# A float32 decoder trunk: all transfers other than weights, input and output issued from the POOL queue instead of SyncE's

## The chip, the cores and the metric

The kernel runs on one core of one Trainium2 chip. The metric is the device time in microseconds of one execution. Three runs of the kernel before the change are given; their median is 1368.77 us (1365.99 to 1369.58).

The core has five instruction queues that run beside each other and wait for one another by semaphores: TensorE (PE, with its weight loads shown as PEld), VectorE (DVE), ScalarE (ACT), GpSimd (POOL) and SyncE (SP), which does no arithmetic and only begins transfers. A transfer is begun by one of the queues and carried out by 16 DMA engines; a queue works in order, so an instruction that waits holds up what is behind it on the same queue.

## The reference

The kernel computes a decoder trunk of two layers over 512 tokens with 1024 features, all in float32. Cut to what matters:

```
def rms_norm(x, w, eps):  return x * rsqrt(mean(x*x, -1) + eps) * w

# layer 0: mixer
h = rms_norm(x, norm_mix[0])
u, q, k, v = split(h @ mix_w_in)                # 512 + 512 + 128 + 128 columns
pooled = [means over 2/4/8/16 trailing tokens of u, minus u] @ pool_w * pool_scale
attn = sliding_window_attention(rope(q), rope(k), v, sinks)     # window 128, 8 heads
x = x + concat(pooled, attn) @ mix_w_out
x = x + conv_ffn(rms_norm(x, norm_ffn[0]))      # (silu(conv(h@up_g)) * conv(h@up_u)) @ down

# layer 1: state space
h = rms_norm(x, norm_mix[1])
z, xbc, dt = split(h @ ssm_w_in)                # xbc: causal convolution of width 4, silu
y = ssd_scan(xs, softplus(dt + bias), -exp(A_log), B, C) + D * xs    # chunks of 128 tokens
x = x + rms_norm(y * silu(z), ssm_norm) @ ssm_w_out
x = x + conv_ffn(rms_norm(x, norm_ffn[1]))
out = rms_norm(x, norm_final)
```

## The kernel before, in words

Everything is kept with the features on the 128 partitions and the 512 tokens along the rows. The residual stream `x` stays in the core's memory as eight tiles of 128x512.

A float32 product is made from exact halves. `load_split` (L131 to L141) loads a weight tile `w` of 128x1024 (512 KB) from SyncE's queue, ScalarE rounds it to `wh` (L139) and VectorE takes the rest `wl` (L140); three buffers are kept of each. `gemm` then issues three matmuls for each of the eight slices (L147 to L149) into one of four PSUM banks with the tag `mm`: 24 matmuls for a tile of 128 features by 512 tokens.

The norm's scale for each token is not needed for a product's inputs. It is applied to the product's result, so the matmuls can run ahead of it. `Stat.add` has ScalarE square a tile and POOL add it up (L172, L173). `Stat.finish` makes the sums over the features by TensorE (L180) and the reciprocal root by a few short VectorE instructions (L184 to L190). The result `rt` holds the tokens along the partitions, 128x4. To get it along the rows on all partitions, `finish` writes it to device memory (`flat<-rt`, L193, 128x4 single elements) and reads it back to all 128 partitions (`rb<-flat`, L195). Six statistics take this way, in order of time: ahead of the mixer, ahead of the first MLP, ahead of the state-space layer, for the norm of y, ahead of the second MLP, and for the first half of the tokens in the final norm. The second half in the final norm takes another way, by TensorE (L199). VectorE multiplies the products by `rb` (L227, L233), which empties the `mm` banks.

The mixer's rotary tables (`rope_tables`) are computed from the positions `pos`, and four copies `L<-L` (L333) spread cosines and sines over the partitions of the two heads. `rope` exchanges halves of a head by four copies `sq<-p` (L356) for the keys and the first two query tiles, by a TensorE product for the others. POOL multiplies by the cosines (L360), VectorE by the sines (L361) and adds (L362). `poolw` (L340) holds the pooling group's weights.

The state-space layer first computes the step sizes (weights `wd`, L514) and the sums over a chunk, and writes these to device memory (`scr`, L564). Then it goes through eight groups; each has six projections of 24 matmuls and a scan over four chunks. Each chunk reads its rows of `scr` to all partitions into `R` (L631, 256 KB, three buffers; `poolw` and the keys use these buffers earlier). VectorE subtracts and clips (L634), ScalarE takes exponentials, POOL multiplies by C (L641) and TensorE sums (L645, L648).

The order of the instructions on each queue is not written by hand. The program is traced once and a planner orders it with a simulated timeline of all queues (`schedule_with_timeline_sim=True`), earlier instructions of the program first where several are ready.

Of the kernel before, what the change touches and what calls it, by code (L numbers as in the profile page):

```python
# [20 lines left out]
P = 128  # L21
# [10 lines left out]
EPS = 1e-6  # L32
SSM_EPS = 1e-5

# columns of the packed per-feature parameters
C_NMIX = 0
C_NFFN = 16
C_NFIN = 32
# [6 lines left out]
C_SD = C_SNW + 16  # L45
NPAR = C_SD + 16

# columns of the constants
K_ID = 0
K_TRI = 128  # L50
K_ONE = 256
# [18 lines left out]
def trunk_kernel(ctx: ExitStack, tc: tile.TileContext, io):  # L70
    nc = tc.nc
    V, A, G, PE = nc.vector, nc.scalar, nc.gpsimd, nc.tensor
# [32 lines left out]
    def yps():  # L105
        return pp.tile([P, T], F32, tag="yp", name=nm("yp"), bufs=2)

# [1 line left out]
    x = cp.tile([P, KD, T], F32, name="x")  # L109
    par = cp.tile([P, NPAR], F32, name="par")  # L110
    con = cp.tile([P, NCON], F32, name="con")
    row = cp.tile([P, 72], F32, name="row")
    nc.sync.dma_start(par[:, :C_NFFN], io["par"][:, :C_NFFN])
    nc.sync.dma_start(x[:, 0, :], io["xT"][:, 0, :])
    # the array's clock and the activation table are up by the time the data is there
    idle = t2("sq", 2)
    G.memset(idle[:], 1.0)
    A.activation(idle[:, 0:1], idle[:, 1:2], AF.Copy)
# [8 lines left out]
    def pc(c):  # L127
        return par[:, c : c + 1]

# [1 line left out]
    def load_split(src, kt=8, cols=P, eng=None):  # L131
        w = wp.tile([P, 8, P], F32, tag="w", name=nm("w"), bufs=3)
        h = wp.tile([P, 8, P], F32R, tag="wh", name=nm("wh"), bufs=3)
# [19 lines left out]
        V.scalar_tensor_tensor(out=l, in0=src, scalar=wcol, in1=h.bitcast(F32),  # L153
                               op0=ALU.mult, op1=ALU.subtract)

# [1 line left out]
    class Stat:  # L157
        def __init__(self, count, width=T, lanes=(G,), late=0):
            self.n, self.w, self.lanes, self.late = 0, width, lanes, count - late
# [15 lines left out]
        def finish(self, dim, eps, copy=True):  # L175
            w, nb = self.w, self.w // P
            ps = aux()
            for c in range(nb):
                for i, part in enumerate(self.parts):
                    PE.matmul(ps[:, c : c + 1], lhsT=part[:, c * P : (c + 1) * P], rhs=ones[:, 0:1],  # L180
                              start=i == 0, stop=i == len(self.parts) - 1)
            sm = tp.tile([P, 4, NB], F32, tag="rt", name=nm("rt"), bufs=2)
            v, s, r, q = (sm[:, i, :nb] for i in range(4))
            V.tensor_scalar(v, ps[:, 0:nb], 1.0 / dim, eps, op0=ALU.mult, op1=ALU.add)  # L184
            A.activation(s, v, AF.Sqrt)
            V.reciprocal(r, s)
            V.tensor_tensor(out=q, in0=r, in1=r, op=ALU.mult)
            V.tensor_tensor(out=q, in0=q, in1=v, op=ALU.mult)
            V.tensor_scalar(q, q, -0.5, 1.5, op0=ALU.mult, op1=ALU.add)
            V.tensor_tensor(out=r, in0=r, in1=q, op=ALU.mult)  # L190
            if copy:
                flat = dp.tile([NB, P], F32, tag="flat", name=nm("flat"), bufs=2)
                nc.sync.dma_start(flat[:nb, :].rearrange("c p -> p c"), r)  # L193
                rb = t2("rb", 1)
                nc.sync.dma_start(rb[:, :w], flat[:nb, :].rearrange("c p -> (c p)").partition_broadcast(P))  # L195
                return rb, r
            pb = aux()
            for c in range(nb):
                PE.matmul(pb[:, c * P : (c + 1) * P], lhsT=r[:, c : c + 1].to_broadcast([P, P]), rhs=ident,  # L199
                          start=True, stop=True)  # L200
            if not copy:
                return pb, r
            rb = t2("rb", 1)
            A.activation(rb[:, :w], pb[:, :w], AF.Copy)
            return rb, r
# [27 lines left out]
        V.tensor_tensor(out=out, in0=ps, in1=rb[:], op=ALU.mult)  # L233

    def conv(src, dst, taps, b):
        """dst = causal depthwise convolution of src; taps oldest first, as columns of par."""
        A.activation(dst, src, AF.Identity, scale=pc(taps[-1]), bias=pc(b))  # L237
        for s in range(1, len(taps)):
            V.scalar_tensor_tensor(out=dst[:, s:], in0=src[:, : T - s], scalar=pc(taps[-1 - s]),  # L239
                                   in1=dst[:, s:], op0=ALU.mult, op1=ALU.add)  # L240

# [1 line left out]
    def finish_out(down, nj, kh, kl):  # L243
        H = T // 2
        warm = tp.tile([P, 1], F32, tag="warm", name="warm", bufs=1)
# [16 lines left out]
                                       in1=scale[half][:, :H], op0=ALU.mult, op1=ALU.mult)  # L262
                nc.sync.dma_start(io["out"][k * P : (k + 1) * P, ts], x[:, k, ts])

# [1 line left out]
    def ffn(layer, cur, nxt):  # L266
        rb, _ = cur.stat.finish(D, EPS)
        up, down = io["wup"], io["wdn"]
# [39 lines left out]
                if part == len(FF_PARTS) - 1:  # L308
                    nxt.tile(n)

# [1 line left out]
    def rope_tables(rb):  # L312
        """The cosines (upper rows) and signed sines (lower rows) of a head, times the tokens' scale."""
        pos = t2("p", 3, I32)
        nc.sync.dma_start(pos[:], io["pos"].partition_broadcast(P))
        ang, n, r = t2("acc", 3), t2("p", 3), t2("L", 3)
        phase, shift, sign = (con[:, K_PH + i : K_PH + i + 1] for i in range(3))
        V.tensor_copy(ang[:], pos[:])
        V.tensor_scalar(ang[:], ang[:], con[:, K_INVF : K_INVF + 1], 0.0, op0=ALU.mult, op1=ALU.add)
        V.tensor_scalar(n[:], ang[:], INV2PI, phase, op0=ALU.mult, op1=ALU.add)  # L320
        V.tensor_scalar(n[:], n[:], MAGIC, MAGIC, op0=ALU.add, op1=ALU.subtract)
        V.scalar_tensor_tensor(out=r[:], in0=n[:], scalar=-PI_C1, in1=ang[:], op0=ALU.mult, op1=ALU.add)
        V.scalar_tensor_tensor(out=r[:], in0=n[:], scalar=-PI_C2, in1=r[:], op0=ALU.mult, op1=ALU.add)
        V.scalar_tensor_tensor(out=r[:], in0=n[:], scalar=-PI_C3, in1=r[:], op0=ALU.mult, op1=ALU.add)
        V.tensor_scalar(r[:], r[:], shift, PI_LIM, op0=ALU.add, op1=ALU.min)
        V.tensor_scalar(r[:], r[:], -PI_LIM, 0.0, op0=ALU.max, op1=ALU.add)
        A.activation(r[:], r[:], AF.Sin, scale=sign)
        V.tensor_tensor(out=r[:], in0=r[:], in1=rb[:], op=ALU.mult)
        res = []
        for half in range(2):  # L330
            t = t2("L", 3)
            for head in range(2):
                nc.sync.dma_start(t[64 * head : 64 * head + 64, :], r[64 * half : 64 * half + 64, :])  # L333
            res.append(t)
        return res

# [1 line left out]
    def mixer(cur, nxt, first_ws):  # L338
        poolw = tp.tile([P, 4, P], F32, tag="R", name="poolw", bufs=3)
        nc.sync.dma_start(poolw[:], io["poolw"])  # L340
        rb, rt = cur.stat.finish(D, EPS)
        hp, lp, ha, la = bt(), bt(), bt(), bt()

# [6 lines left out]
        def rope(ps, dst, by_dma):  # L350
            f = t2("p", 3)
            A.activation(f[:], ps[:], AF.Copy)
            if by_dma:
                src = t2("sq", 2)
                for b in range(4):
                    nc.sync.dma_start(src[32 * b : 32 * b + 32, :], f[32 * (b ^ 1) : 32 * (b ^ 1) + 32, :])  # L356
            else:
                src = yps()
                PE.matmul(src[:], lhsT=swap, rhs=f[:], start=True, stop=True)
            G.tensor_tensor(out=dst[:], in0=f[:], in1=cos[:], op=ALU.mult)  # L360
            V.tensor_tensor(out=f[:], in0=src[:], in1=sin[:], op=ALU.mult)  # L361
            V.tensor_tensor(out=dst[:], in0=dst[:], in1=f[:], op=ALU.add)  # L362

        # causal pooling
        def pool(g, w):
            ps = project(g)
            ub = ct()
# [18 lines left out]
        cos, sin = rope_tables(rb)  # L386
        k = ct()
        rope(project(8), k, True)
        # each key head alone, the other's rows zero, so that the products span all rows
        kz = [tp.tile([P, T], F32, tag="R", name=nm("kz"), bufs=3) for _ in range(2)]  # L390
        for p in range(2):
            rows, rest = slice(p * 64, (p + 1) * 64), slice((1 - p) * 64, (2 - p) * 64)
# [12 lines left out]
        for j in range(4):  # L405
            ps = project(4 + j)
            q.append(ct())
            rope(ps, q[j], j < ROPE_DMA)
        # banded attention, two heads groups of four; heads j and 4+j share tile j
        mask = con[:, K_MASK : K_MASK + 256]  # L410
        def scores(n):
            k0 = 0 if n else P
# [50 lines left out]
            A.activation(hh, o4, AF.Copy)  # L463
            V.tensor_tensor(out=ll, in0=o4, in1=hh.bitcast(F32), op=ALU.subtract)

        # the pooled half of the output product and the attention's first tokens run beside the attention
        def out_pooled(n2):
            ws = load_split(io["wmo"][0, n2])
            for i in range(2):
# [36 lines left out]
            out_attn(n, wa[n], slice(T // 2, T))  # L506
            nxt.tile(n)

# [1 line left out]
    def ssm(cur, nxt):  # L510
        rb, rt = cur.stat.finish(D, EPS)
        # step sizes, token-major [token, chunk, head]: four column groups, each over a quarter of the features
        wd = wp.tile([P, KD, NH], F32, tag="w", name="wd", bufs=3)
        nc.sync.dma_start(wd[:], io["wdt"])  # L514
        wn = par[:, C_NMIX + 8 : C_NMIX + 16].unsqueeze(2).to_broadcast([P, KD, NH])
        V.tensor_tensor(out=wd[:], in0=wd[:], in1=wn, op=ALU.mult)
        dfm = mm()
# [10 lines left out]
        dt, av, acs, dec, dbc, e1, e2 = (sd[:, i, :] for i in range(7))  # L528

        def v3(a):  # L530
# [3 lines left out]
        V.tensor_tensor(out=v3(dt), in0=v3(dt), in1=rt.unsqueeze(2).to_broadcast([P, NB, NH]), op=ALU.mult)  # L534
        V.tensor_tensor(out=v3(dt), in0=v3(dt), in1=row[:, 0:NH].unsqueeze(1).to_broadcast([P, NB, NH]),
                        op=ALU.add)
        # softplus(v) = max(v, 0) + 2 atanh(e / (2 + e)), e = exp(-|v|)
        A.activation(e1, dt, AF.Abs)
        A.activation(e1, e1, AF.Exp, scale=-1.0)
        V.tensor_scalar(e2, e1, 2.0, 0.0, op0=ALU.add, op1=ALU.add)  # L540
# [20 lines left out]
        A.activation(dbc, ps[:, P : 2 * P], AF.Exp)  # L561
        V.tensor_copy(e1, ps[:, 2 * P : 3 * P])
        scr = dp.tile([P, P], F32, name="scr")
        nc.sync.dma_start(scr[:], e1)  # L564

        stat = Stat(16)
        y4 = [bt(F32) for _ in range(4)]
# [16 lines left out]
        for g in range(GROUPS):  # L584
# [42 lines left out]
            for c in range(NB):  # L627
                cs = slice(c * P, (c + 1) * P)
                h0 = c * NH + 4 * g
                R = tp.tile([P, 4, P], F32, tag="R", name=nm("R"), bufs=3)  # L630
                nc.sync.dma_start(R[:], scr[h0 : h0 + 4, :].partition_broadcast(P))  # L631
                L = tp.tile([P, 4, P], F32, tag="L", name=nm("L"), bufs=3)
                for r in range(4):
                    V.tensor_scalar(L[:, r, :], R[:, r, :], acs[:, h0 + r : h0 + r + 1], 0.0,  # L634
# [26 lines left out]
            for t in range(2):  # L661
                f = 2 * g + t
# [107 lines left out]
```

## Time and profile before

| What | Value |
|---|---|
| Runs | 1365.99, 1368.77, 1369.58 us, median 1368.77 |
| Profiled execution | span 1366.1 us; its time outside the profile is not given apart from it |
| PE busy | 1311.2 us, 96% |
| DVE busy | 887.5 us, 65% |
| ACT busy | 597.5 us, 44% |
| POOL busy | 161.2 us, 12%, 117 instructions |
| Transfers | 134.30 MB, mean 98 GB/s, all from SyncE's queue |

The span is cut by a page into busy shares, a chain of work that ended last, groups of instructions by line, and transfers. In a group, `out<-in` are the program's names without buffer numbers. In a timeline, the columns are the start and the duration in us, the engine, the line and the operation; the bracket gives the idle time ahead of it and what ended that. "SPq" is SyncE's queue, whose rows are the issues of transfers; "issue" is time in which an engine waited for nothing that the profile shows. PEclk is the clock that was granted to TensorE, 1.00 being full speed.

### The profile page before, as it was taken

How to read it: one execution, taken by the hardware profiler on the slowest of the kernel's cores; microseconds unless marked ns; L12 is line 12 of the kernel's file. 1: busy time of each engine (PE TensorE's matmuls, PEld its weight loads, DVE VectorE, ACT ScalarE, POOL GpSimd, SP SyncE). 2: the span in 40 equal slices, each digit the busy share in tenths (PEclk: the TensorE clock that was granted, in tenths of full speed). 3: DMA queues.
4: the chain of work that ended last, by engine and by line, in shares of the span. 5: the costliest groups of instructions: out<-in, count | busy, mean ns of one | idle time of the engine just before them, and what ended most of it. 6: DMA issues, size and time to landing. Idle time of an engine off the chain costs nothing.

```text
span 1366.1 us, 16570 instructions
## 1 busy us (share of the span) xinstructions
PE 1311.2 (96%) x6398; PEld 1073.4 (79%) x6398; DVE 887.5 (65%) x1364; ACT 597.5 (44%) x826; POOL 161.2 (12%) x117
## 2 busy tenths in 40 slices
PE   8799999999999999899999999997999999999995
PEld 5576978888888887778888888676878888888895
DVE  5674548547646764678888878854567467557763
ACT  5364235324424443465666655632344234334451
POOL 3213020000000002012321313211100000000021
PEclk9899999999999999999999999999999999999998
DMA  6313113233233323253333333212333333233352
GB/s 223 103 37 93 63 39 119 93 103 102 81 105 104 95 88 102 70 132 109 100 109 103 98 120 97 91 64 85 93 87 97 102 99 96 92 101 103 96 155 81
DMA packets 46511, 134.30 MB, mean 98 GB/s; under 512 B 8160, under 2 KB 10592, under 8 KB 46432
## 3 DMA queue, kind: packets, MB, share of 16 engines
q1 hardware_dynamic: 46432, 133.25, 32.1%
q8 instruction: 50, 0.82, 0.2%
q14 instruction: 29, 0.24, 0.1%
HBM read 129.74 MB, written 2.17 MB: 97 GB/s over the span
## 4 chain that ended last, share of the span: by engine, by line
PE 85%; DMA 6%; DVE 4%; issue 2%; ACT 2%; POOL 0%; SPq 0%; DVEq 0%; ACTq 0%; POOLq 0%
PE mm L149 26%; PE mm L147 26%; PE mm L148 26%; DMA flat<-rt 3%; DMA rb<-flat 2%; DVE wl L140 1%; PE yp L645 1%; PE yp L453 1%; PE mm L420 1%; DMA R<-scr 1%; PE ax L459 1%; ACT wh L139 1%; PE yp L648 1%; PE ax L651 1%; DVE c L239 1%
## 5 line engine op out<-in xcount | busy, mean ns | idle before, releaser
L147 PE MATMUL mm<-a,wh 128*128 128x512 f32 x1232 | 486.4, 396 | 19.9 <-DVE p L227 7.8
L149 PE MATMUL mm<-a,wl 128*128 128x512 f32 x1232 | 486.6, 395 | 3.6 <-DVE wl L140 3.6
L148 PE MATMUL mm<-a,wh 128*128 128x512 f32 x1232 | 485.3, 394 | 3.4 <-DVE a L153 3.4
L139 ACT ACTIVATE wh<-w 128x1024 fp32r<-128x1024 f32 (+1 forms) x221 | 229.0, 1041 | 411.7 <-PE mm L148 366.4
L140 DVE TENSOR_TENSOR wl<-w,wh 128x1024 fp32r<-128x1024 f32 (+1 forms) x222 | 281.6, 1271 | 78.3 <-ACT wh L139 77.1
L147 PEld LDWEIGHTS mm<-a,wh 128*128 128x128 f32 x1232 | 233.3, 189 | 73.1 <-issue 21.8
L149 PEld LDWEIGHTS mm<-a,wl 128*128 128x128 f32 x1232 | 233.0, 189 | 56.8 <-DVE wl L140 6.7
L148 PEld LDWEIGHTS mm<-a,wh 128*128 128x128 f32 x1232 | 233.1, 189 | 56.3 <-DVE a L153 7.2
L173 POOL TENSOR_TENSOR sacc<-sacc,sq 128x512 f32<-128x512 f32 (+1 forms) x53 | 82.2, 1552 | 907.7 <-ACT sq L172 906.2
L233 DVE TENSOR_TENSOR p<-mm,rb 128x512 f32<-128x512 f32 x120 | 82.4, 689 | 100.2 <-PE mm L149 79.1
L239 DVE SCALAR_TENSOR_TENSOR acc<-p,par,acc 128x511 f32<-128x511 f32 (+1 forms) x176 | 131.1, 748 | 3.1 <-ACT acc L237 0.3
L149 PE MATMUL mm<-b,wl 128*128 128x512 f32 (+1 forms) x272 | 92.4, 344 | 6.1 <-DVE wl L140 6.1
L230 DVE TENSOR_TENSOR x<-mm,x 128x512 f32<-128x512 f32 x48 | 32.4, 689 | 98.0 <-PE mm L149 98.0
L148 PE MATMUL mm<-b,wh 128*128 128x512 f32 (+1 forms) x272 | 93.7, 346 | 0.0
L148 PE MATMUL mm<-c,wh 128*128 128x512 f32 x240 | 93.3, 390 | 0.0
L147 PE MATMUL mm<-b,wh 128*128 128x512 f32 (+1 forms) x272 | 92.0, 345 | 1.0 <-ACT wh L139 1.0
L147 PE MATMUL mm<-c,wh 128*128 128x512 f32 x240 | 92.3, 390 | 0.5 <-ACT c L152 0.5
L149 PE MATMUL mm<-c,wl 128*128 128x512 f32 x240 | 92.6, 389 | 0.0
L237 ACT ACTIVATE acc<-p,par 128x512 f32<-128x512 f32 x88 | 71.0, 809 | 31.1 <-DVE p L233 30.6
L239 DVE SCALAR_TENSOR_TENSOR c<-p,par,c 128x511 f32<-128x511 f32 (+2 forms) x96 | 75.3, 784 | 1.6 <-ACT c L237 0.4
L296 ACT ACTIVATE acc<-acc 128x512 f32<-128x512 f32 x44 | 27.8, 633 | 80.8 <-DVE acc L239 80.8
L149 PEld LDWEIGHTS mm<-b,wl 128*128 128x128 f32 x272 | 52.6, 194 | 12.1 <-DVE wl L140 6.3
(185 smaller groups left out, 1276.6 us busy)
## 6 DMA issues: line engine op xcount, KB each, us to landing
w<-wup SPq DMA_DIRECT2D x88, 512.0 KB, 3.5
w<-wsi SPq DMA_DIRECT2D x48, 512.0 KB, 3.5
w<-wdn SPq DMA_DIRECT2D x32, 448.0 KB, 3.2
w<-wdn SPq DMA_DIRECT2D x24, 512.0 KB, 3.5
R<-scr SPq DMA_DIRECT2D x32, 256.0 KB, 3.5
w<-wso SPq DMA_DIRECT2D x16, 512.0 KB, 3.6
w<-wmi SPq DMA_DIRECT2D x10, 512.0 KB, 4.0
w<-wmo SPq DMA_DIRECT2D x8, 512.0 KB, 3.5
```

Of the source, the lines that this page charges most:

```text
L139: A.activation(h[:, :kt, :cols], w[:, :kt, :cols], AF.Copy)
L140: V.tensor_tensor(out=l[:, :kt, :cols], in0=w[:, :kt, :cols], in1=h[:, :kt, :cols].bitcast(F32), op=ALU.subtract)
L147: PE.matmul(ps, lhsT=h[:, k, :], rhs=rh[k][:, ts], start=first and k == 0, stop=False)
L148: PE.matmul(ps, lhsT=h[:, k, :], rhs=rl[k][:, ts], start=False, stop=False)
L149: PE.matmul(ps, lhsT=l[:, k, :], rhs=rh[k][:, ts], start=False, stop=last and k == kt - 1)
L173: self.lanes[lane].tensor_tensor(out=acc[:, :w], in0=acc[:, :w], in1=sq[:, :w], op=ALU.add)
L230: V.tensor_tensor(out=x[:, n, :], in0=ps[:], in1=x[:, n, :], op=ALU.add)
L233: V.tensor_tensor(out=out, in0=ps, in1=rb[:], op=ALU.mult)
L237: A.activation(dst, src, AF.Identity, scale=pc(taps[-1]), bias=pc(b))
L239: V.scalar_tensor_tensor(out=dst[:, s:], in0=src[:, : T - s], scalar=pc(taps[-1 - s]), in1=dst[:, s:], op0=ALU.mult, op1=ALU.add)
L296: A.activation(g[:], g[:], AF.Silu)
L420: PE.matmul(s[:, j, k0:], lhsT=q[2 * jj + j][:, n * P : (n + 1) * P], rhs=kz[p][:, n * P + k0 - P : (n + 1) * P], start=True, stop=True)
```

## The change

Every transfer that isn't a weight tile of a large product, the input or the output is begun by POOL (`G.dma_start`) where it was begun by SyncE (`nc.sync.dma_start`). What stays on SyncE: all loads of `w`, the input `x`, the constants `con`, `par` and `row`, and the stores of `out`. The pieces below are the whole change; other differences are in comments only.

```diff
 # Stat.finish
-                nc.sync.dma_start(flat[:nb, :].rearrange("c p -> p c"), r)
+                G.dma_start(flat[:nb, :].rearrange("c p -> p c"), r)
                 rb = t2("rb", 1)
-                nc.sync.dma_start(rb[:, :w], flat[:nb, :].rearrange("c p -> (c p)").partition_broadcast(P))
+                G.dma_start(rb[:, :w], flat[:nb, :].rearrange("c p -> (c p)").partition_broadcast(P))
 # rope_tables
-        nc.sync.dma_start(pos[:], io["pos"].partition_broadcast(P))
+        G.dma_start(pos[:], io["pos"].partition_broadcast(P))
...
-                nc.sync.dma_start(t[64 * head : 64 * head + 64, :], r[64 * half : 64 * half + 64, :])
+                G.dma_start(t[64 * head : 64 * head + 64, :], r[64 * half : 64 * half + 64, :])
 # mixer, rope
-        nc.sync.dma_start(poolw[:], io["poolw"])
+        G.dma_start(poolw[:], io["poolw"])
...
-                    nc.sync.dma_start(src[32 * b : 32 * b + 32, :], f[32 * (b ^ 1) : 32 * (b ^ 1) + 32, :])
+                    G.dma_start(src[32 * b : 32 * b + 32, :], f[32 * (b ^ 1) : 32 * (b ^ 1) + 32, :])
 # ssm
-        nc.sync.dma_start(wd[:], io["wdt"])
+        G.dma_start(wd[:], io["wdt"])
...
-        nc.sync.dma_start(scr[:], e1)
+        G.dma_start(scr[:], e1)
...
-                nc.sync.dma_start(R[:], scr[h0 : h0 + 4, :].partition_broadcast(P))
+                G.dma_start(R[:], scr[h0 : h0 + 4, :].partition_broadcast(P))
```

## The prediction

> **What bounds the kernel now.** I read the page's busy shares first, then the chain that ended last, then TensorE's timeline for every idle stretch, the waits of the SyncE queue, and last the transfers.
>
> ```profile
> span 1366.1 us, 16570 instructions
> ...
> PE 1311.2 (96%) x6398; PEld 1073.4 (79%) x6398; DVE 887.5 (65%) x1364; ACT 597.5 (44%) x826; POOL 161.2 (12%) x117
> ```
>
> TensorE is busy 96% of the span: 1366.1 - 1311.2 = 54.9 us are idle. Nothing but that idle time, and TensorE's clock, can be won back; a delay elsewhere costs only where TensorE ends up waiting.
>
> ```profile
> 205.00:540.00 335.00, 335.00 (x1485) 276.07 (x1484) 214.09 (x267) 133.02 (x167) 10.98 (x7) 1.00 0.32 98
> ...
> 575.00:850.00 275.00, 271.95 (x1528) 223.22 (x1527) 227.58 (x413) 162.23 (x208) 64.19 (x38) 1.00 0.36 108
> ```
>
> The columns are the stretch, its length, and the busy time of PE, PEld, DVE, ACT and POOL. In the first stretch (all the gated MLP's inner part) PE is busy 335.00 of 335.00 us, in the second (most of the state-space scan) 271.95 of 275.00, at a granted clock of 1.00. Weights arrive in time there, so transfers taken off SyncE's queue free nothing.
>
> ```profile
> SPq L135 <- DVE wl L140: 915.3, 189, 21.3
> SPq L195 <- DMA flat<-rt: 49.1, 6, 9.3
> ```
>
> The queue of SyncE (SPq) spends 915.3 us waiting until a weight buffer is free, which no other queue changes. It stands 49.1 us, six times, behind `flat<-rt`: the same queue waits for that transfer before it may begin `rb<-flat`, and weight loads stand behind both.
>
> ```profile
> PE 85%; DMA 6%; DVE 4%; issue 2%; ACT 2%; POOL 0%; SPq 0%; DVEq 0%; ACTq 0%; POOLq 0%
> PE mm L149 26%; PE mm L147 26%; PE mm L148 26%; DMA flat<-rt 3%; DMA rb<-flat 2%; DVE wl L140 1%; PE yp L645 1%; PE yp L453 1%; PE mm L420 1%; DMA R<-scr 1%; PE ax L459 1%; ACT wh L139 1%; PE yp L648 1%; PE ax L651 1%; DVE c L239 1%
> ```
>
> The chain is 85% PE; the moved transfers `flat<-rt`, `rb<-flat` and `R<-scr` hold 3%, 2% and 1% of it. These are TensorE's idle stretches that the moved transfers touch (start, duration, group, and in brackets the idle time before it and what ended it):
>
> ```profile
> 42.28 0.76 PE L147 MATMUL mm<-a,wh 128*128 128x512 f32 x1 [6.07 <-DVE c L233]
> ...
> 44.51 0.79 PE L149 MATMUL mm<-a,wl 128*128 128x512 f32 x1 [1.04 <-DVE wl L140]
> ...
> 75.88 4.13 PE L420 MATMUL mm<-kz,c 128*128 128x128 f32 x16 [2.10 <-DVE c L362]
> ...
> 199.57 0.47 PE L147 MATMUL mm<-a,wh 128*128 128x512 f32 x1 [2.10 <-DVE p L233]
> ...
> 565.28 0.50 PE L149 MATMUL mm<-a,wl 128*128 128x512 f32 x1 [0.93 <-DVE wl L140]
> ...
> 595.88 1.16 PE L620 MATMUL ax<-c,c 128*128 128x128 f32 x8 [1.82 <-ACT c L582]
> ...
> 930.14 0.77 PE L147 MATMUL mm<-a,wh 128*128 128x512 f32 x1 [7.83 <-DVE p L227]
> ...
> 1001.26 0.77 PE L147 MATMUL mm<-a,wh 128*128 128x512 f32 x1 [3.29 <-DVE p L233]
> ...
> 1343.62 0.58 PE L149 MATMUL mm<-b,wl 128*128 128x256 f32 x1 [6.13 <-DVE wl L140]
> ```
>
> Five of them stand right behind a `rb` of the six statistics (Stat.finish, L193 and L195). The first is 6.07 us, with 1.04 behind it where `wl` came late; then 2.10 at 199.57, 7.83 at 930.14, 3.29 at 1001.26, and 6.13 at 1343.62. The third statistic shows only 0.93 at 565.28. I call them F1 to F6 in order of time: F1 7.1, F2 2.1, F3 0.9, F4 7.8, F5 3.3, F6 6.1, together 27.3 us, half of all idle time. TensorE has run ahead until its four `mm` banks are full, and VectorE's product with `rb` (L227, L233) empties them. So each microsecond by which `rb` comes later is one of TensorE's.
>
> **What is moved.** The transfers, with KB each and the median us from issue to landing:
>
> ```profile
> R<-scr SPq DMA_DIRECT2D x32, 256.0 KB, 3.5
> ...
> rb<-flat SPq DMA_DIRECT2D x5, 256.0 KB, 4.2
> sq<-p SPq DMA_DIRECT2D x12, 64.0 KB, 2.0
> L<-L SPq DMA_DIRECT2D x4, 128.0 KB, 2.3
> ...
> poolw<-poolw SPq DMA_DIRECT2D x1, 256.0 KB, 6.4
> p<-pos SPq DMA_DIRECT2D x1, 256.0 KB, 6.3
> wd<-wdt SPq DMA_DIRECT2D x1, 128.0 KB, 2.3
> rb<-flat SPq DMA_DIRECT2D x1, 128.0 KB, 4.5
> flat<-rt SPq DMA_DIRECT2D x5, 2.0 KB, 9.1
> scr<-sd SPq DMA_DIRECT2D x1, 64.0 KB, 3.1
> ...
> flat<-rt SPq DMA_DIRECT2D x1, 1.0 KB, 7.5
> ```
>
> That is 32+5+12+4+1+1+1+1+5+1+1 = 64 transfers. They no longer stand in SyncE's queue among the weight loads, but in POOL's, among its 117 instructions. No transfer is added or removed. What is new: POOL must issue them, its arithmetic stands behind them, and while `rb` waits in POOL's queue for `flat` to land, so does all that is behind it. After each of F1 to F5 POOL's next work itself needs `rb`, and POOL is 12% busy, so that wait I cost at nothing; its cover is VectorE's wait for the same `rb`.
>
> **The price of a transfer issued by POOL.** No row of this trace shows one. Downwards it is bounded by SyncE's own price, and by what a queue of its own could save:
>
> ```profile
> 915.65 9.69 DMA flat<-rt
> ...
> 1329.17 7.49 DMA flat<-rt
> ```
>
> The longest `flat` (9.69) stood behind weight loads, the shortest (7.49) less so: at best 2.2 us are saved. Upwards, POOL's nearest row of work over 512 elements is
>
> ```profile
> L173 POOL TENSOR_TENSOR sacc<-sacc,sq 128x512 f32<-128x512 f32 (+1 forms) x53 | 82.2, 1552 | 907.7 <-ACT sq L172 906.2
> ```
>
> 1552 ns on average. `flat<-rt` is 128x4 = 512 separate elements, half that in F6, and someone has to describe each. If POOL needs one such pass, `flat` lands 1.55 us later; with two words for the reading and two for the writing side, four passes, 6.2. A transfer of 128 rows has a quarter of this: 0.4, at most 1.6. I take one pass, as the row is the only one nearby, and 0.5 of the 2.2 for the queue. A statistic then comes 1.55 + 0.4 - 0.5 = 1.45, say 1.5 us later (from -2.2 to +7.8).
>
> The Trainium skill (DMA: Bandwidth & Descriptors, section "Latency and other measured facts") gives a first byte after about 1 us for transfers issued by GpSimd and about 0.6 for those of sync and scalar, which speaks against this change. By that, an estimate: 0.4 for each of the two transfers of a statistic, 0.8 instead of 1.5 in each of six, and the sum below would be 4.2 us lower. No run here shows it yet.
>
> **The sum, stage by stage.**
>
> The clock belongs to it. Stretches behind F2, F5 and F6; the value after POOL's count is the granted clock:
>
> ```profile
> 199.50:209.00 9.50, 9.43 (x42) 7.83 (x43) 8.59 (x12) 7.27 (x9) 0.00 (x0) 1.00 0.18 55
> ...
> 1001.00:1005.00 4.00, 3.74 (x10) 3.04 (x11) 4.00 (x7) 3.85 (x5) 0.00 (x0) 0.57 0.02 7
> ...
> 1343.60:1350.50 6.90, 6.88 (x36) 6.88 (x37) 5.51 (x10) 1.25 (x3) 3.05 (x3) 0.58 0.35 112
> ```
>
> After 2.10 us idle the clock stayed at 1.00. After 3.29 it was 0.57 over 4.0 us, a loss of 4.0 x 0.43 = 1.7 us. After 6.13 it was 0.58 over 6.9 us, a loss of 2.9.
>
> F1: +1.5, less the 1.04 that `wl` came late, since its weights no longer stand behind `rb`: +0.5. F2: its stall grows from 2.1 to 3.6, past F5's, so the clock's 1.7 is added: +3.2. F3, F4, F5: +1.5 each. F6: +1.5 if VectorE's order stays (see the rivals). Together 9.7.
>
> The rotary tables: POOL's product with the cosines waits for four copies.
>
> ```profile
> 56.91 2.43 SPq L333 DMA_DIRECT2D L<-L  x4
> ```
>
> SyncE issues four in 2.43 us, 0.61 each. Describing (0.4) comes on top for the last of them at least and for all four at most, +0.4 to +1.6; I take +0.9. The four `sq<-p` of the following rope hold POOL for another 2.4 to 4.0 us between its own products, which VectorE's rope sums and with them `wl` wait for; a third of 3 I count, +1.0. The path leads to the 2.10 us at 75.88, so +1.9; from 0 to +6.
>
> State space, start: `scr`, then the first `R`, then the third behind two others (+0.4, +0.4, +0.7) lead through VectorE's queue to the 1.82 us at 595.88: +1.5, from 0 to +5. Between there and its end PE is 99% busy, so later `R` loads are covered by matmuls of the next group; if that cover went, VectorE would be late with `wl` next. At the end two `R` loads are in the chain, 0.4 each, +0.8:
>
> ```profile
> 849.04 3.24 DMA R<-scr
> ```
>
> `poolw` and `pos` will go out early on an idle POOL and collide with the first tiles of x; `wd` has slack. I take 0, and at most +2, half of the 4.2 us that a 256 KB transfer takes.
>
> Sum: 9.7 + 1.9 + 1.5 + 0.8 = 13.9 us. Against the profiled execution (span 1366.1; no other own time of it is given) this is 1380.0. The median of the three runs, 1368.77, is 2.7 above that span and their lowest, 1365.99, just below it, so in the median's terms I forecast 1368.8 + 13.9 = 1382.7. About 0.3%, 4.1 us, is what can be told from no change.
>
> **The rivals.**
>
> *Faster: the last weights overtake the norm.* In F6 TensorE waits for a `wl` that stands behind three scalings in VectorE's queue, and these wait for `rb`:
>
> ```profile
> 1341.16 1.27 DVE L261 SCALAR_TENSOR_TENSOR x<-x,par,rb 128x256 f32<-128x256 f32 x3 [9.20 <-DMA rb<-flat]
> 1342.35 1.22 DVE L140 TENSOR_TENSOR wl<-w,wh 128x1024 fp32r<-128x1024 f32 x1
> ```
>
> SyncE begins the last weight load right behind `rb`:
>
> ```profile
> 1337.10 0.38 SPq L135 DMA_DIRECT2D w<-wdn  x1
> ```
>
> The instruction order comes from a planner that simulates the queues. With the weights free of `rb` it may place `wl` ahead of the scalings, which come later in the program. Then 6.13 us of stall and 2.9 of clock go, 9.0 in all, and the 1.5 isn't paid. For it: the weights' dependence on `rb` is really removed. Against: `w` for the blocked `wl` had landed earlier, and the planner put the scalings first all the same. It decides the sign once all other terms sum to less than 9.0 - 4.1 = 4.9 us. With POOL's transfers at SyncE's price the rest is F1's -1.0, so -10.0: 1358.8. With my prices it is 13.9 - 1.5 - 9.0 = +3.4: 1372.2, no change.
>
> *Much slower: describing elements is dear.* At four passes a statistic costs 7.8: six times 7.8, the rope's 6, the scan's 5 and F2's 1.7 give +59.5: 1428. For it: 512 elements of 4 bytes are the worst shape there is. Against: `flat` takes 7.5 us with 256 elements and 9.1 with 512, so most of its time isn't in their number. It starts to decide at two passes (+3.5 each, about +25).
>
> *Much faster: POOL's transfers land quickly.* If `flat` and `rb` took what the quickest moved transfers take (`sq<-p`, 2.0 us), each statistic would be over 8 us earlier and all six stalls would go, with the clock's 1.7 and 2.9: -32, 1337. Against: four-byte writes stay what they are whoever issues them. The Trainium skill (DMA: Bandwidth & Descriptors, section "Anatomy of one DMA") states for a transfer from GpSimd about 2.0 us plus its bytes over 436 GB/s, which would be this case, 2.0 and 2.6 us here; the 9.1 and 4.2 us of the trace, from SyncE, are far from it.
>
> *Hidden anyway.* The 64 transfers cost POOL what they cost SyncE and the order stays: only F1's 1.04 moves, no change. It shares its outcome with the third sum above.
>
> **How the numbers follow.** My forecast (order kept, about one pass; +6 to +22, 1375 to 1391): 0.45. Dear elements: 0.13. No change (overtaking at my prices, or hidden anyway): 0.20, of which a quarter ends above 0.3%. Overtaking at SyncE's prices: 0.17. Quick landing: 0.05. Slower: 0.45 + 0.13 + 0.05 = 0.63; same 0.15; faster 0.17 + 0.05 = 0.22. The range leaves out quick landing and most of the dear case: from 1356, below the overtaking's 1358.8, to 1400.
>
> **What would show it.** A DMA row with POOLq for 64 transfers, in place of SPq. `flat` near 10 us and `rb` near 4.6 to landing (forecast right), above 13 (dear), or near 2 (quick). TensorE's six idle stretches: F2 above 3 us with a clock near 0.6 behind it, F1 without the 1.04. F6 tells the overtaking: `wl` ahead of the scalings in VectorE's timeline and no idle stretch there. For the rope, the idle stretch ahead of the first scores, 2.10 us before, near 4; for the scan, 1.82 near 3.3. The prediction would be wrong above all through the planner: a new order on VectorE or TensorE in stages that hold no moved transfer moves time in either direction, and nothing in this profile sizes it.

## The result and the profile after

| Kernel | Median, us | Runs | Span of the profiled execution, us |
|---|---|---|---|
| before | 1369.17 | 1365.99 to 1369.73 (4) | 1366.1 |
| after | 1381.63 | 1380.32 to 1382.88 (4) | 1378.6 |

The changed kernel is slower: the ratio is 1.0094, with a 95% interval from 1.0079 to 1.0108. That is 12.5 us, in the medians and in the spans alike. Forecast were 13.9.

From the page of the changed kernel come its span, its busy shares, and a second queue of transfers that the page of before did not have:

```profile
span 1378.6 us, 16581 instructions
...
PE 1316.0 (95%) x6398; PEld 1076.1 (78%) x6398; DVE 888.1 (64%) x1364; ACT 600.8 (44%) x828; POOL 199.0 (14%) x181
...
q0 software_dynamic: 4016, 11.88, 3.3%
```

TensorE's idle time grew from 54.9 to 1378.6 - 1316.0 = 62.6 us, by 7.7. The other 4.8 us are in its busy time, with the same 6398 matmuls: some ran at a lower clock. The line of queue q0 says that the move took place: 4016 packets now go another way.

The transfers of the changed kernel (KB each, median us from issue to landing):

```profile
R<-scr POOLq DMA_DIRECT2D x32, 256.0 KB, 3.6
...
x<-xT SPq DMA_DIRECT2D x8, 256.0 KB, 7.3
...
rb<-flat POOLq DMA_DIRECT2D x5, 256.0 KB, 4.4
sq<-p POOLq DMA_DIRECT2D x12, 64.0 KB, 2.3
L<-L POOLq DMA_DIRECT2D x4, 128.0 KB, 3.7
...
flat<-rt POOLq DMA_DIRECT2D x5, 2.0 KB, 9.1
scr<-sd POOLq DMA_DIRECT2D x1, 64.0 KB, 2.7
...
flat<-rt POOLq DMA_DIRECT2D x1, 1.0 KB, 9.1
```

In the rows of before, `R` took 3.5, `rb` 4.2, `sq` 2.0, `scr` 3.1, `L` 2.3. From POOL these land within 0.4 us of that, on either side, but for `L` (3.7). `flat` of five statistics lands in 9.1 as before; that of the sixth, with 256 elements, in 9.1 where it took 7.5. One row changed although it was not moved, the input's. Before it read:

```profile
x<-xT SPq DMA_DIRECT2D x8, 256.0 KB, 5.6
```

TensorE's idle stretches in the changed kernel (start, duration, group; in brackets the idle time ahead of it and what ended that):

```profile
45.12 0.77 PE L147 MATMUL mm<-a,wh 128*128 128x512 f32 x1 [5.91 <-DVE c L233]
...
77.27 0.49 PE L420 MATMUL mm<-kz,c 128*128 128x128 f32 x2 [2.52 <-DVE c L362]
...
203.62 0.47 PE L147 MATMUL mm<-a,wh 128*128 128x512 f32 x1 [3.66 <-DVE p L233]
...
570.48 0.47 PE L147 MATMUL mm<-a,wh 128*128 128x512 f32 x1 [1.18 <-DVE c L233]
...
600.43 1.16 PE L620 MATMUL ax<-c,c 128*128 128x128 f32 x8 [1.84 <-ACT c L582]
...
938.21 0.76 PE L147 MATMUL mm<-a,wh 128*128 128x512 f32 x1 [8.01 <-DVE p L227]
...
1011.61 0.77 PE L147 MATMUL mm<-a,wh 128*128 128x512 f32 x1 [5.22 <-DVE p L233]
...
1354.69 0.48 PE L147 MATMUL mm<-b,wh 128*128 128x256 f32 x1 [3.07 <-ACT wh L139]
...
1359.65 0.58 PE L149 MATMUL mm<-b,wl 128*128 128x256 f32 x1 [4.27 <-DVE wl L140]
```

F1 is 5.91 (6.07 before) and the 1.04 behind it is gone. F2 is 3.66 (2.10), F3 1.18 (0.93), F4 8.01 (7.83), F5 5.22 (3.29). F6 is 3.07 + 4.27 = 7.34 (6.13). The stall ahead of the scores is 2.52 (2.10), that at L620 1.84 (1.82). Set beside the starts of the same groups before, these rows say where the time was lost:

| Stretch | Before, us | After, us | Longer by | Forecast |
|---|---|---|---|---|
| start until TensorE resumes behind F1 | 42.28 | 45.12 | 2.84 | 0.5 |
| on to the resumption behind F2 (mixer) | 157.29 | 158.50 | 1.21 | 3.4 |
| on to that behind F4 (first MLP, scan) | 730.57 | 734.59 | 4.02 | 7.0 |
| on to that behind F5 (norm of y) | 71.12 | 73.40 | 2.28 | 1.5 |
| on to the end (second MLP, F6) | 364.84 | 366.99 | 2.15 | 1.5 |

The forecast of a stretch adds its terms of the prediction: F1; rope and F2's stall; F2's clock, F3, the scan's 2.3 and F4; F5; F6. The sums agree to 1.4 us, the stretches less well: three are longer than forecast, by 2.3, 0.8 and 0.7, and two shorter, by 2.2 and 3.0.

### The profile page after: what moved, and what is told of

Same layout as the page of the kernel before. It is cut to its first block, busy times and chain, and to the rows that moved or that the text cites. A ratio compares the mean times of both kernels' runs of the same rounds, so it can differ in the third digit from the quotient of the medians.

```text
span 1378.6 us, 16581 instructions
## 1 busy us (share of the span) xinstructions
PE 1316.0 (95%) x6398; PEld 1076.1 (78%) x6398; DVE 888.1 (64%) x1364; ACT 600.8 (44%) x828; POOL 199.0 (14%) x181
## 3 DMA queue, kind: packets, MB, share of 16 engines
q0 software_dynamic: 4016, 11.88, 3.3%
## 5 line engine op out<-in xcount | busy, mean ns | idle before, releaser
L148 PE MATMUL mm<-a,wh 128*128 128x512 f32 x1232 | 487.9, 396 | 3.5 <-DVE a L153 3.3
L140 DVE TENSOR_TENSOR wl<-w,wh 128x1024 fp32r<-128x1024 f32 (+1 forms) x222 | 273.0, 1233 | 85.8 <-ACT wh L139 84.5
L148 PEld LDWEIGHTS mm<-a,wh 128*128 128x128 f32 x1232 | 233.8, 190 | 57.9 <-DVE a L153 7.8
L148 PE MATMUL mm<-b,wh 128*128 128x512 f32 (+1 forms) x272 | 93.6, 346 | 0.0
L148 PE MATMUL mm<-c,wh 128*128 128x512 f32 x240 | 93.6, 391 | 0.0
L239 DVE SCALAR_TENSOR_TENSOR c<-p,par,c 128x511 f32<-128x511 f32 (+2 forms) x96 | 80.2, 839 | 1.6 <-ACT c L237 0.4
L147 PEld LDWEIGHTS mm<-b,wh 128*128 128x128 f32 x272 | 52.4, 194 | 11.1 <-ACT wh L139 4.7
```

The costliest lines, as they stand in the source:

```text
L140: V.tensor_tensor(out=l[:, :kt, :cols], in0=w[:, :kt, :cols], in1=h[:, :kt, :cols].bitcast(F32), op=ALU.subtract)
L147: PE.matmul(ps, lhsT=h[:, k, :], rhs=rh[k][:, ts], start=first and k == 0, stop=False)
L148: PE.matmul(ps, lhsT=h[:, k, :], rhs=rl[k][:, ts], start=False, stop=False)
```

## The experiments

Each is a ratio to the kernel before on the same chip; the us are that ratio's excess times the median of before there (1371.64 for the first four kernels, 1372.72 for the next four, 1372.29 for the rest).

| Kernel | What it is | Ratio, 95% | us |
|---|---|---|---|
| stat_only | before, `flat` and `rb` from POOL | 1.0077 (1.0065 to 1.0089) | +10.6 |
| start_only | before, `poolw` and `pos` from POOL | 1.0035 (1.0023 to 1.0047) | +4.8 |
| rope_only | before, `L` and `sq` from POOL | 1.0013 (1.0001 to 1.0026) | +1.8 |
| scan_only | before, `wd`, `scr`, `R` from POOL | 1.0007 (0.9996 to 1.0019) | +1.0 |
| after_again | the changed kernel | 1.0099 (1.0078 to 1.0120) | +13.6 |
| after_stat_sp | it, `flat` and `rb` back on SyncE | 1.0044 (1.0027 to 1.0062) | +6.0 |
| held | it, `poolw` and `pos` held back | 1.0083 (1.0063 to 1.0103) | +11.4 |
| pe_stat | before, statistics by TensorE | 0.9765 (0.9745 to 0.9785) | -32 |
| rows_pool | stat_only, `flat` in rows | 0.9763 (0.9746 to 0.9779) | -33 |
| rows_sp | before, `flat` in rows | 0.9782 (0.9768 to 0.9796) | -30 |
| flat_pool | before, `flat` alone from POOL | 1.0033 (1.0022 to 1.0043) | +4.5 |
| pe_rest_pool | pe_stat, the other transfers from POOL | 0.9749 (0.9735 to 0.9763) | -34 |

**One part of the change at a time.** My theory after the result was that the change costs where a moved transfer ends a wait of TensorE's, above all in the six statistics. The rival was that the planner's new order costs the time, wherever it falls.

`stat_only`:

```diff
-                nc.sync.dma_start(flat[:nb, :].rearrange("c p -> p c"), r)
+                G.dma_start(flat[:nb, :].rearrange("c p -> p c"), r)
-                nc.sync.dma_start(rb[:, :w], flat[:nb, :]...)
+                G.dma_start(rb[:, :w], flat[:nb, :]...)
```

> The kernel before with flat<-rt and rb<-flat alone (12 transfers) issued by POOL. Theory A (the later rb costs, one for one, plus TensorE's clock behind the longer stalls): +8 us against before (1377), of it 3 at the second and 3 at the fifth statistic, each stall there about 1.5 to 2 us longer. Theory B (the planner's new order costs, the transfers hardly): +3 us or less, as the order of this kernel differs from before in few places on TensorE.

Measured: +10.6 us, most of the whole change, from 12 of 64 transfers. Its transfers, and two of TensorE's idle stretches:

```profile
rb<-flat POOLq DMA_DIRECT2D x5, 256.0 KB, 4.3
...
flat<-rt POOLq DMA_DIRECT2D x5, 2.0 KB, 9.5
```

```profile
202.70 0.77 PE L147 MATMUL mm<-a,wh 128*128 128x512 f32 x1 [4.58 <-DVE p L233]
...
937.20 0.77 PE L147 MATMUL mm<-a,wh 128*128 128x512 f32 x1 [8.79 <-DVE p L227]
```

F2 is 4.58 against 2.10 before, F4 8.79 against 7.83. The statistics cost as the first theory has it, and more than its 8 us; the prediction had 9.7.

`start_only`:

```diff
-        nc.sync.dma_start(pos[:], io["pos"].partition_broadcast(P))
+        G.dma_start(pos[:], io["pos"].partition_broadcast(P))
...
-        nc.sync.dma_start(poolw[:], io["poolw"])
+        G.dma_start(poolw[:], io["poolw"])
```

> The kernel before with poolw and pos alone issued by POOL; orders of TensorE and VectorE are unchanged. Theory A (they go out at 1.3 us and take the DMA engines from the first tiles of x): +2.8 us (1372), the second tile of x lands 2 us later. Theory B (the 2.8 us of the first stage come from elsewhere, the statistic among them): less than +0.7 us.

Measured: +4.8 us, where the prediction had taken 0. The order of TensorE's and VectorE's instructions is that of before, so a new order is no cause here. TensorE resumes behind F1 at 45.16 us, against 42.28 before; where the rest of the 4.8 arises I have not isolated. The input's row tells the cause of the 2.9 us; it is 7.6 against 5.6 before:

```profile
x<-xT SPq DMA_DIRECT2D x8, 256.0 KB, 7.6
```

`rope_only` moves `t[64...]` and `src[32...]`, `scan_only` moves `wd`, `scr` and `R`, by the same exchange of `nc.sync` for `G` in those lines.

> The kernel before with the twelve sq<-p and four L<-L alone issued by POOL. Theory A (they are covered): within 1 us of before. Theory B (my forecast's: POOL's products stand behind them): +1.9 us, with the idle stretch ahead of the first scores near 4 us instead of 2.1.

> The kernel before with wd, scr and the 32 R<-scr alone issued by POOL. Theory A (R is covered by matmuls except at the scan's start and end): +1 to +2 us, no new idle stretch above 1.5 us between 600 and 850. Theory B (the planner's other order on TensorE and VectorE in the scan costs): +4 us or more, as this kernel has most of the changed order.

Measured: +1.8 us, hardly told from nothing, and +1.0 us, not told from nothing. In `scan_only` 34 transfers are moved and many of TensorE's instructions stand in a new order. So a new order by itself need not cost anything. The four parts add to 18.2 us, the whole to 12.9 (1.0094) or 13.6 (1.0099): they don't simply add up. The intervals leave 1.6 to 1.7 us either way on each part and 2.9 on the whole. Put together as independent errors, an estimate, that is 4.4, so the 4.6 between 18.2 and 13.6 is barely told from nothing, and I haven't found a cause.

**The whole change again, with one part undone.** `after_again` is the changed kernel itself, for comparison on the same chip. `after_stat_sp` puts the statistics back:

```diff
 # Stat.finish of the changed kernel
-                G.dma_start(flat[:nb, :]..., r)
+                nc.sync.dma_start(flat[:nb, :]..., r)
-                G.dma_start(rb[:, :w], flat[:nb, :]...)
+                nc.sync.dma_start(rb[:, :w], flat[:nb, :]...)
```

> The changed kernel once more, beside its variants. Both theories: +12.5 us against before, as measured (ratio 1.008 to 1.011). The four parts alone gave +10.6, +4.8, +1.8 and +1.0, 18.2 together; if that sum were real and the parts only add up, this would be +18.

> The changed kernel with flat<-rt and rb<-flat back on SyncE; all 52 other transfers stay on POOL. Theory A (the six statistics carry most of the loss): +3 to +6 us against before, 7 to 10 less than the changed kernel, stalls behind the statistics as before (7.1, 2.1, 0.9, 7.8, 3.3, 6.1). Theory B (the other transfers and the planner's new order carry it): +9 or more.

Measured: +13.6 and +6.0 us, so the statistics carry 7.6 within the whole change (the intervals leave some 4 us on either side, so this doesn't differ from the 10.6 alone). TensorE's timeline of `after_stat_sp`:

```profile
47.33 0.80 PE L149 MATMUL mm<-a,wl 128*128 128x512 f32 x1 [1.04 <-DVE wl L140]
...
205.25 0.77 PE L147 MATMUL mm<-a,wh 128*128 128x512 f32 x1 [3.63 <-DVE p L233]
...
1011.91 0.47 PE L147 MATMUL mm<-a,wh 128*128 128x512 f32 x1 [3.25 <-DVE p L233]
```

The 1.04 us in which TensorE waits for `wl` behind F1 is back, as the weights wait again behind `rb`, and F5 is 3.25 (3.29 before, 5.22 in the changed kernel). F2 at 3.63 did not go back to 2.10; its spread between executions is told below.

**The start.** `held` makes each of the two early transfers wait for the last tile of the input, by a write of one column to its target:

```diff
+        V.tensor_copy(pos[:, 0:1], x[:, KD - 1, 0:1])
         G.dma_start(pos[:], io["pos"].partition_broadcast(P))
...
+        A.activation(poolw[:, 0, 0:1], x[:, KD - 1, 0:1], AF.Copy)
         G.dma_start(poolw[:], io["poolw"])
```

> The changed kernel, but poolw and pos may begin only when the last tile of x has landed (a one-column write that depends on x is put ahead of each). Theory A (at the start the two transfers, 512 KB, delay the tiles of x on the DMA engines): first stage 2.5 to 3 us shorter than in the changed kernel, +9.5 us against before. Theory B (the start is later through the order of ScalarE's and POOL's queue): no difference from the changed kernel.

Measured: +11.4 against +13.6 us, with intervals that overlap. POOL's timeline is plainer:

```profile
14.46 0.68 POOL L316 DMA_DIRECT2D p<-pos  x1
...
16.38 0.55 POOL L342 DMA_DIRECT2D poolw<-poolw  x1
...
29.34 0.78 POOL L193 DMA_DIRECT2D flat<-rt  x1 [6.02 <-DVE rt L190]
```

The two now start at 14.46 and 16.38. The input's tiles land in 5.6 us again, and the first `flat` starts at 29.34, against 31.52 in `after_again` and 27.98 before: 2.2 of the 3.5 us lost there came back. That the early transfers delay the input is shown. TensorE resumes behind F1 at 44.16 against 45.99, so 1.8 us reach that point, behind a stretch of 6.85 against 6.50; that they reach the end is not shown.

**Is it POOL, or the elements?** The prediction put the price down to POOL describing 512 elements. `pe_stat` takes the way through device memory out of all six statistics: the product with the identity that the final norm's second half uses, and a copy by ScalarE, serve for all.

```diff
-            if copy:
-                flat = dp.tile([NB, P], F32, tag="flat", ...)
-                nc.sync.dma_start(flat[:nb, :].rearrange("c p -> p c"), r)
-                rb = t2("rb", 1)
-                nc.sync.dma_start(rb[:, :w], flat[:nb, :]...)
-                return rb, r
             pb = aux()
             ... PE.matmul(pb[...], lhsT=r[...].to_broadcast([P, P]), rhs=ident, ...)
```

> The kernel before with no flat and no rb transfer at all: each of the six statistics is spread over the partitions by TensorE (a product with the identity, as the last half already does) and copied by ScalarE; all other transfers stay on SyncE. Theory A (TensorE's stalls behind the statistics are the 13 us on the way through device memory): the six stalls, 27 us, and about 6 of lost clock go, less about 1 us for each new product and copy: -20 us against before, 1349 to 1354. Theory B (VectorE's order and the mm banks hold TensorE there anyway): -5 us or less.

Measured: -32 us, 1339.63 us, more than either theory had. From its page:

```profile
span 1337.8 us, 16643 instructions
...
PE 1311.6 (98%) x6442; PEld 1073.1 (80%) x6442; DVE 887.9 (66%) x1364; ACT 600.0 (45%) x831; POOL 152.6 (11%) x117
```

TensorE is idle for 1337.8 - 1311.6 = 26.2 us, against 54.9 before; none of the six stretches is left.

`rows_pool` and `rows_sp` keep the way through device memory and the same 2 KB, and write them as 128 rows of 16 bytes. Each token then gets another token's scale, so these two kernels do not compute the reference's result and serve the time alone:

```diff
-                ....dma_start(flat[:nb, :].rearrange("c p -> p c"), r)
+                ....dma_start(flat[:nb, :].rearrange("c p -> (c p)").rearrange("(p c) -> p c", c=nb), r)
```

> As stat_only (flat and rb issued by POOL), but flat is written as 128 rows of 16 bytes instead of 512 single elements, so each token gets another token's scale; the orders of TensorE, VectorE, ScalarE and SyncE are those of stat_only. Theory A (POOL's describing of 512 elements is what is dear, as the prediction's step has it): POOL's issue falls from 0.78 to about 0.55 us and flat lands 1.5 us sooner than in stat_only or more, near 8; the statistics cost less than +4 us against before. Theory B (the time lies in the small writes to device memory, whoever describes them): flat stays within 0.5 us of stat_only's 9.5, +8 to +10.5 us.

> The kernel before, all transfers on SyncE, with flat written as 128 rows of 16 bytes (each token gets another token's scale). Theory A (number of elements): flat lands in about 3 us like scr<-sd (128 rows of 512 bytes, 3.1 us) instead of 9.1; the kernel gains 15 us or more. Theory B (small writes to one stretch of device memory): flat stays above 7 us, the gain is below 6 us.

Measured: -33 us (1338.69) from POOL, which neither theory had, and -30 us (1342.37) from SyncE. The order of TensorE's, VectorE's, ScalarE's and SyncE's instructions in `rows_pool` is that of `stat_only`. The transfers of `rows_pool`, then two of its idle stretches:

```profile
flat<-rt POOLq DMA_DIRECT2D x5, 2.0 KB, 2.5
```

```profile
37.67 0.47 PE L147 MATMUL mm<-a,wh 128*128 128x512 f32 x1 [1.66 <-DVE c L233]
...
910.84 0.47 PE L147 MATMUL mm<-a,wh 128*128 128x512 f32 x1 [2.68 <-DVE p L227]
```

F1 is 1.66 and F4 2.68, where `stat_only` had 5.93 and 8.79. The transfers of `rows_sp`:

```profile
flat<-rt SPq DMA_DIRECT2D x5, 2.0 KB, 3.1
```

`flat` lands in 2.5 us from POOL (9.5 in `stat_only`) and in 3.1 from SyncE (9.1 before). The form of the write makes 6 to 7 us of the 9, whoever issues it. Whether it is the number of pieces, their 4 bytes, or their being spread over memory, these runs don't tell apart. The Trainium skill (DMA: Bandwidth & Descriptors, section "Rules for kernel authors") says that a transfer whose last dimension isn't contiguous becomes one descriptor for each element, and to rearrange it. The trace agrees where SyncE issues: `rows_sp` has 6112 packets under 512 bytes and before 8160, and the 2048 between them are 2816 elements (five times 512 and 256) less 768 rows. From POOL the queue has 640 packets in `stat_only` and in `rows_pool` alike, so there the number of packets does not explain 9.5 against 2.5 us. The Trainium skill has no figure there for the price of an element.

**Which of the two transfers.** `flat_pool` moves `flat` alone and leaves `rb` on SyncE:

```diff
-                nc.sync.dma_start(flat[:nb, :].rearrange("c p -> p c"), r)
+                G.dma_start(flat[:nb, :].rearrange("c p -> p c"), r)
```

> The kernel before with flat<-rt alone issued by POOL and rb<-flat by SyncE. Theory A (the price of a statistic lies in flat, as 10.0 against 8.7 us from its issue to rb's shows): +8 us or more, like stat_only's +10.6. Theory B (half of it lies in rb, which meets weight loads once SyncE is free): +3 to +5 us.

Measured: +4.5 us, somewhat under half of `stat_only`'s 10.6. So about half goes with `flat`, half with `rb`. Its rows:

```profile
rb<-flat SPq DMA_DIRECT2D x5, 256.0 KB, 4.6
...
flat<-rt POOLq DMA_DIRECT2D x5, 2.0 KB, 9.0
```

`rb` from SyncE lands in 4.6 us here, from POOL in 4.3 in `stat_only`, counted from the start of its issue: what moving `rb` costs is not in its landing. Part of it lies ahead of the issue. In the chain of `stat_only`, at F4:

```profile
922.03 9.47 DMA flat<-rt
...
932.06 4.28 DMA rb<-flat
```

`flat` has landed at 931.50 and POOL begins `rb` at 932.06, 0.56 later, and the profile names nothing that it waits for. SyncE's row of before, behind the `flat` that began at 915.65 and took 9.69, that is until 925.34:

```profile
925.36 0.33 SPq L195 DMA_DIRECT2D rb<-flat  x1
```

That is 0.02 us. In all kernels here with `rb` from POOL this gap is 0.29 to 0.56 us at each statistic, in all with `rb` from SyncE, `flat_pool` too, 0.01 to 0.02. Six times 0.45 us, the mean difference between these two kernels, is 2.7, an estimate, of the 6 us between them; the rest I haven't found.

**The other transfers without the statistics.** `pe_rest_pool` is `pe_stat` with the other 52 transfers begun by POOL, so the start, rope and scan parts of the change.

> As pe_stat (no flat and rb; 32 us faster than before), with the other 52 transfers of the change issued by POOL. Theory A (they cost by themselves, as after_stat_sp's +6.0 and the +4.8 of the start say): +5 to +7 us against pe_stat, -26 against before. Theory B (they cost only through the stalls and the clock behind the statistics): within 2 us of pe_stat.

Measured: 1337.97 us, the lowest median of all that ran. Beside `pe_stat`'s 1339.63 (another chip, its ratio 0.9765) the 52 transfers cost nothing on the whole, though the same 52 cost +6.0 in `after_stat_sp`, where the statistics are slow. That does not mean that each of them is free. The same group of TensorE's in `pe_stat` and then in `pe_rest_pool`:

```profile
546.26 0.60 PE L519 MATMUL ax<-con,p 128*128 128x128 f32 x4
```

```profile
548.94 0.60 PE L519 MATMUL ax<-con,p 128*128 128x128 f32 x4
```

The tiles of the input land in 7.5 us again (5.8 in `pe_stat`), and TensorE is 2.7 us behind, as it is already at the first statistic (L180, 27.14 against 24.37): the early `poolw` and `pos` cost here about what they cost in the changed kernel. It is made up in and behind the scan, where `pe_stat` has five idle stretches above 0.8 us, 6.8 us together, and `pe_rest_pool` two, 3.6 together. That the planner's order there is the reason is not shown. So the second theory's number came, and its reason, that these transfers cost only through the stalls behind the statistics, did not hold at the start.

## Why the prediction was right

1382.7 was forecast, 1381.63 came, and the sign and most of the size hang on the step that was to carry them: the six statistics, 9.7 us forecast, 7.6 (within the change) to 10.6 (alone) measured. That the total comes within 1.4 us is in part luck: the start was taken at 0 and cost 2.84 in the changed kernel (4.8 alone), the rope and the scan were taken at 4.2 and cost 2.8 alone, and the price of a statistic was about right for a wrong reason.

*F1 to F6.* The wait for `wl` behind F1 went as said, and F2 passed into the clock's reach. The stretch behind F2 in the changed kernel (the columns are those of the prediction's stretches; the granted clock stands third from the end):

```profile
203.60:208.00 4.40, 4.38 (x12) 3.47 (x13) 4.40 (x7) 3.08 (x4) 0.00 (x0) 0.61 0.27 56
```

The clock is 0.61 over 4.4 us, a loss of 4.4 x 0.39 = 1.7, the figure forecast; before it had been 1.00 there. The idle time grew by -0.16 at F1 (-1.20 with the 1.04 that went), 1.56 at F2, 0.25 at F3, 0.18 at F4, 1.93 at F5 and 1.21 at F6. That is 3.9 us together, where the forecast without the clock's 1.7 has 8.0, and far from 1.5 for each. A later `rb` was not always TensorE's loss one for one: at F3 the time from the issue of `flat` to that of `rb` grew by 1.82 us (next paragraph) and the stretch by 0.25.

*The price of one statistic.* From the issue of `flat` to that of `rb` the six took 9.20, 7.90, 8.14, 9.71, 9.08 and 7.50 us before, and 9.32, 8.83, 9.96, 9.97, 9.61 and 9.62 after: +0.96 on average (from +0.12 to +2.12), against 1.55 - 0.5 = 1.05 in the sum. Of F1's the rows are these, of POOL in the changed kernel and of SyncE before:

```profile
1.29 0.68 POOL L340 DMA_DIRECT2D poolw<-poolw  x1
...
1.97 0.55 POOL L315 DMA_DIRECT2D p<-pos  x1
...
31.24 0.78 POOL L193 DMA_DIRECT2D flat<-rt  x1 [8.82 <-DVE rt L190]
...
40.56 0.54 POOL L195 DMA_DIRECT2D rb<-flat  x1 [8.54 <-DMA flat<-rt]
```

```profile
9.94 0.33 SPq L340 DMA_DIRECT2D poolw<-poolw  x1
...
10.60 0.33 SPq L315 DMA_DIRECT2D p<-pos  x1
...
27.98 0.38 SPq L193 DMA_DIRECT2D flat<-rt  x1
...
37.18 0.33 SPq L195 DMA_DIRECT2D rb<-flat  x1
```

Over the kernels here that write single elements, the mean of the six is 8.46 to 9.11 us where SyncE begins both transfers (five kernels), 9.55 to 10.23 where POOL does (four), and 9.12 in `flat_pool`: moving both costs some 1 us each time, though one statistic alone moves as much by itself.

The size was right and its reason was not. POOL's issue takes 0.78 us for `flat` and 0.54 for `rb`; SyncE's took 0.38 and 0.33. Describing 512 elements rather than 128 rows thus costs POOL 0.24 us more where the prediction had 1.55 against 0.4. The +0.96 has two parts: `flat` lands 0.57 us later, counted from the start of its issue, of which the longer issue is 0.40; and POOL begins `rb` 0.41 us after that landing on average, SyncE 0.02. Why POOL takes that long stays open. The 0.5 that a queue of its own was to save does not show: from the end of its issue `flat` took 8.19 us on average before and 8.36 after. The bound of 2.2 behind it had compared a `flat` of 512 elements with the one of 256. By the Trainium skill's figures for the first byte (DMA: Bandwidth & Descriptors, "Latency and other measured facts") the forecast would have been 4.2 us lower, 1378.5; the rows of the plain transfers agree with a difference of that kind in part (`sq` +0.3, `rb` +0.2, `R` +0.1), `scr` (-0.4) does not.

*The start: 0 taken, 2.84 measured.* This was the one term that was plainly mis-sized, and outside its bound of +2. The rows above show `poolw` and `pos` go out at 1.29 and 1.97, where SyncE had them at 9.94 and 10.60, behind the input. The collision was foreseen and its price was not: a tile of the input lands at 7.3 instead of 5.6 us, and all that leads to the first statistic is late.

*The rope (+1.9) and the scan (+2.3).* The idle stretch ahead of the scores went from 2.10 to 2.52 and not to 4, that at L620 from 1.82 to 1.84 and not to 3.3. But TensorE's timeline of the changed kernel has idle time close by that the prediction did not name:

```profile
78.47 0.80 PE L420 MATMUL mm<-kz,c 128*128 128x128 f32 x2 [0.71 <-DVE c L362]
...
606.69 0.70 PE L651 MATMUL ax<-XD,c 128*128 128x256 f32 x2 [1.21 <-POOL XD L615]
...
874.96 0.50 PE L148 MATMUL mm<-a,wh 128*128 128x512 f32 x1 [2.00 <-DVE a L153]
```

Before there was none at the first two, and 0.92 at the third (865.83). So the rope's stretches grew by 1.1 us and the scan's by 2.3, as much as was forecast for it and at other places. The stretch at L148 is 2.00 to 2.52 us in each kernel that has the single elements and `R` from POOL, and 0.6 to 1.1 in those with `R` from SyncE; through which wait `R` leads to it is not shown. Measured alone, both parts cost +1.8 and +1.0, barely or not told from nothing. Counting POOL's description of rows at 0.4 a transfer was too dear; the issue is 0.2 longer than SyncE's.

*The rivals.* The overtaking did not happen. The end of the chain in the changed kernel:

```profile
1350.31 4.86 DMA rb<-flat
1355.61 2.85 DVE x L261 x7
1358.46 1.15 DVE wl L140
```

Seven scalings (L261) of this chain stand between `rb` and the last `wl`, where the prediction's line of before has three ahead of it: the planner's order went the other way. The dear elements did not come: `flat` from issue to landing is 9.1 us, not 13. The quick landing, 1337, did not come from POOL; but its working, that six quick statistics are worth 32 us, was right: 1338.7, 1342.4 and 1339.6 came once the elements were rows, or gone. The sentence "most of its time isn't in their number" was drawn from 256 elements at 7.5 us and 512 at 9.1. The runs don't tell whether it is wrong, as the rows differ in number, size and layout at once; but it would have kept a reader from the change that pays.

## What to carry to other kernels

The queue that begins a transfer mattered here by about 1 us where its landing ended a wait, and elsewhere by little that these runs can tell from nothing; the form of the transfer mattered by 6 us. So look first for transfers of single elements on the path, and write them as rows or keep them off device memory. Of these two, only the second was done here with the right scales (`pe_stat`); the rows would need the tokens in that order, which no run here tried. A transfer moved to an idle queue also starts earlier, and may then delay the input that everything waits for.

## What the runs showed of the hardware

2 KB written as 512 single 4-byte elements landed after 8.3 to 9.8 us (medians of the kernels), as 128 rows of 16 bytes after 2.5 to 3.1. One statistic with the same two transfers from SyncE, F2, took 7.90 us from the issue of `flat` to that of `rb` before, 8.92 in `rope_only` and 10.56 in `after_stat_sp`. TensorE's stall behind it was 2.10, 3.39 and 3.63 us. The granted clock over the 4.4 us behind that stall was 1.00, 0.67 and 0.68; in `flat_pool` it was 1.00 behind 3.19 us. Between the landing of `flat` and the start of the issue of `rb` lay 0.01 to 0.02 us on SyncE's queue and 0.29 to 0.56 on POOL's, in every kernel here with both transfers.
